# A two-layer diffusion transformer block: TensorE's order in the attention stage written in the source, and both heads' scores in one tile of three PSUM banks

## The chip, the core and the metric

The kernel runs on one core of a Trainium2 chip. The metric is the device time of one execution in microseconds (us). The core's engines run beside each other and meet at semaphores: TensorE (PE, its weight loads apart as PEld), VectorE (DVE), ScalarE (ACT), GpSimd (POOL) and SyncE (SP), which issues the DMAs. TensorE writes its results to PSUM, 8 banks of 512 float32 columns on 128 partitions; VectorE and ScalarE read them there. Each engine works its instructions off in order, so an instruction that waits holds up all behind it on its engine.

## The reference, cut to what matters

Two layers over 512 latent and 256 context tokens, width 1024. One projection of the normed tokens feeds attention (8 query heads, 2 key heads of 64), a pooling branch, a Fourier branch, and a sigmoid gate for each of the three. The attention that the change touches:

```python
h = modulate(rms_norm(x, norm_mix[l]), sh1, sc1)
k, v, q, u, f, gt = jnp.split(h @ w_in[l], IN_SPLITS, axis=-1)
q = apply_rope(q, cos, sin); k = apply_rope(k, cos, sin)
# per query block of 128: own block and its neighbours, |distance| <= 128, and all 256 context keys
s_all = concatenate([where(valid, q @ k_band, NEG_INF), q @ k_ctx, sink]) # scaled by 1/8
p = softmax(s_all)
o = p_lat @ v_band + p_ctx @ v_ctx
y = (g_a * (o @ w_br_attn) + g_p * (pool(u) @ w_br_pool) + g_f * (fourier(f) @ w_br_four))
x = x + g1 * (y @ w_out)
```

In the first layer the context tokens are queries too and read context keys alone. In the second they only give keys and values.

## The kernel before

Activations lie transposed, features on the partitions and the 768 tokens along the columns. A weight tile of 128x1024 comes by one DMA (`wraw`) and is split in two parts of a shorter format, `whi` on ACT (L323) and `wlo` mostly on DVE (L324). A projection runs in steps over the contraction (k steps), each of three matmuls (L346: high x high, high x low, low x high), 512 columns for the latent tokens and 256 for the context, into a PSUM bank from `bank()` (`mp`, or `mm` in stages that have it).

The attention stage of a layer takes the four query tiles t (two heads each) and the query blocks n: 24 units in layer 0 (six blocks, two of them context), 16 in layer 1. A query tile is projected, copied out of PSUM on ACT (L541), rotated (L544 to L547, one of them on GpSimd) and split into high and low parts (L559, L560). A unit then goes like this:

- scores (L602 to L614): for each head, two matmuls against 256 context keys, two against the band of 256 or 384 latent keys, and one or two matmuls that add a mask. A context unit has the first two alone. A unit is 512 or 640 columns wide, or 256 for context;
- softmax: the maximum on DVE (L617), a few small operations (L621, L623), the exponential on ACT (L627) with its sum read off, and the normalisation on DVE (L634);
- turning: each 128 columns of probabilities are transposed on TensorE into the one `tp` bank (L649), four at a time, and copied to SBUF by ACT or DVE (L651, L653);
- values: matmuls of 128 columns for both heads into the `pv` bank (L658), copied out by ACT (L662).

`attn_q` runs two query tiles at a time, and a gate with its Fourier branch (`br_gate`: 8 of them, "filler") is emitted after every third unit in layer 0 and every second in layer 1. The program order is only a start: a scheduler orders the instructions of every engine by its own costs, TensorE's too, so that projections come between the parts of a unit. PSUM in this stage: `sc` has two tiles of two banks, one for each head's scores (L599, `bufs` 2), `tp` and `pv` one bank each, and `mp` two for projections.

Of the kernel before, what the change touches and what calls it, by code (L numbers as in the profile page):

```python
# [17 lines left out]
P = 128  # L18
# [17 lines left out]
SBB = dict(p=2, pt=3)  # L36
# [8 lines left out]
    + tuple((s, (i,), (6, 7)) for i in range(3) for s in "LC"),  # L45
)
# [19 lines left out]
def _plan(l):  # L66
# [12 lines left out]
    fill, gf = [], gates("w_brf", 18, 4)  # L79
    for m in range(8):  # L80
        fill.append([next(gf) for _ in range(1 + (m % 4 == 0))])
    blocks, per = (6, 3) if l == 0 else (4, 2)
    unit = 0
    for half in range(2):
        yield from tiles(6 + 2 * half, 7 + 2 * half)
        for _ in range(2 * blocks):
            unit += 1
            if unit % per == 0 and fill:
                yield from fill.pop(0)
    for f in fill:  # L90
        yield from f
# [17 lines left out]
class Lazy:  # L109
# [6 lines left out]
    def __getitem__(self, i):  # L116
        if self.t[i] is None:
            self.t[i] = self.make()
        return self.t[i]


class Kern:
# [26 lines left out]
    def phase(self, ps, sb):  # L149
        for c in reversed(self.scopes):  # L150
            c.__exit__(None, None, None)
        self.scopes = []
        self.nph += 1
        if ps:
            self.pst, self.sbt = ps, sb
            self.scopes = [
                self.tc.tile_pool(name=f"ps{self.nph}", bufs=1, space=bass.MemoryType.PSUM),
                self.tc.tile_pool(name=f"tp{self.nph}", bufs=1),
            ]
# [358 lines left out]
    def br_gate(self, l, m, mg, br, hs, ls, gh, gl, streams, y, first, steps=0):  # L518
        nc = self.nc
        outs = self.in_tile(l, mg, gh, gl, streams)  # L520
        w, wof = br
        for (b, c0, c1, ps) in outs:
# [4 lines left out]
            self.mm3(pb, w, wof, hs, ls, (c0, c1))  # L527
# [5 lines left out]
        if steps:  # L533
            self.step(last, steps)

# [14 lines left out]
    def attn_q(self, l, t, hs, ls, streams):  # L550
        nc = self.nc
        outs = self.in_tile(l, 6 + t, hs, ls, streams)
        c1 = max(o[2] for o in outs)
        r = self.rope(outs)
        qs = self.slots(2)
        for h in range(2):
            own, oth = (slice(0, 64), slice(64, 128)) if h == 0 else (slice(64, 128), slice(0, 64))
            q = qs[h][:, 0 : c1]
            nc.scalar.copy(q[own], r[own, :c1])  # L559
            nc.vector.tensor_tensor(q[oth], r[own, :c1], q[own].bitcast(F32), ALU.subtract)  # L560
        return qs
# [24 lines left out]
    def scores(self, l, t, n, qs, ka, kb):  # L586
        nc = self.nc
        ps, mx = [], self.small(2)
        if n < 4:
            b0, b1 = max(n - 1, 0), min(n + 1, 3)  # L590
            q0 = n * P
            bl = (b1 - b0 + 1) * P
        else:
            q0 = n * P
            bl = 0
        k0 = b0 * P if n < 4 else 0
        w = bl + CT
        for h in range(2):
            s = self.bk("sc", 1024)[:, 512 - bl : 512 + CT]  # L599
            q = qs[h][:, q0 : q0 + P]  # L600
            cx = s[:, bl:w]
            nc.tensor.matmul(cx, q, ka[h][:, T : N], start=True, stop=False)  # L602
            nc.tensor.matmul(cx, q, kb[h][:, T : N], start=False, stop=True)
            if bl:
                bd = s[:, 0:bl]
# [29 lines left out]
        chunks = ([b0 + j for j in range(bl // P)] if bl else []) + [4, 5]  # L635
        return pr, chunks, q0

    def pv(self, st, vs, o):
        nc = self.nc
        pr, chunks, q0 = st  # L640
        nch = len(chunks)
        pts = []
        for h in range(2):
            pt = self.tmp("pt", 640)
            for j0 in range(0, nch, 4):
                j1 = min(j0 + 4, nch)
                tpb = self.bk("tp", (j1 - j0) * P)
                for j in range(j0, j1):
                    nc.tensor.transpose(tpb[:, (j - j0) * P : (j - j0 + 1) * P], pr[h][:, j * P : (j + 1) * P], self.ident)  # L649
                if (h + j0 // 4) % 2 == 0:  # L650
                    nc.scalar.copy(pt[:, j0 * P : j1 * P], tpb)  # L651
                else:
                    nc.vector.tensor_copy(pt[:, j0 * P : j1 * P], tpb)  # L653
            pts.append(pt)
        po = self.bk("pv", P)
        for j, c in enumerate(chunks):
            for h in range(2):
                nc.tensor.matmul(  # L658
                    po[64 * h : 64 * h + 64, :], vs[:, c * P + 64 * h : c * P + 64 * h + 64],
                    pts[h][:, j * P : (j + 1) * P], start=(j == 0), stop=(j == nch - 1), tile_position=(0, 64 * h),  # L660
                )
        nc.scalar.copy(o[:, q0 : q0 + P], po)  # L662

    def layer(self, l, xs, streams, h=None, after=None):
# [95 lines left out]
        self.phase(dict(sc=2, tp=1, pv=1), SBB)  # L760
        o = self.slots(4, F32)
        gf = iter(range(8))
        wf = [None]

        def filler():
            m = next(gf, None)
            if m is None:
                return
            if m % 4 == 0:
                wf[0] = self.weights("w_brf", l, m // 4)  # L770
            br = (wf[0], lambda k, mm=m: ((mm % 4) * 2 + k) * P)
            self.br_gate(l, m, 18 + m, br, fhi, flo, hs, ls, streams, y[m], False)

        nblk = ncol // P
        units = 0
        per = 3 if nblk > 4 else 2
        for half in range(2):
            ts = (2 * half, 2 * half + 1)
            qs = {t: self.attn_q(l, t, hs, ls, streams) for t in ts}
            prev = None  # L780
            for t in ts:
                for n in range(nblk):
                    st = (self.scores(l, t, n, qs[t], ka, kb), o[t])
                    if prev:
                        self.pv(prev[0], vs, prev[1])
                    prev = st
                    units += 1
                    if units % per == 0:
                        filler()
# [303 lines left out]
```

## Time and profile before

| | |
|---|---|
| median of 3 runs | 1897.43 us (1896.26 to 1898.76) |
| profiled execution, first to last instruction (span) | 1894.8 us |
| median less span | 2.6 us |
| TensorE busy | 1848.8 us, 98% of the span |
| DVE / ACT busy | 65% / 36% |
| attention stage, layer 0, first score to last value product | 205 to 402 us |
| attention stage, layer 1 | 1257 to 1399 us |
| TensorE's granted clock, mean | 0.992 |

The page gives no time of the profiled execution apart from its span; the 2.6 us stand for what lies around it. A start time in a timeline is in us from the span's start. "Idle before, releaser" is time an engine stood before an instruction, and what ended it. TensorE's records are pipelined, so one matmul's pace is read from start to start and not from its length.

### The profile page before, as it was taken

The numbers are of one execution on the slowest core, as the hardware profiler recorded it, in microseconds if no ns is written. First come the engines' busy times: TensorE is split into PE (matmuls) and PEld (weight loads), VectorE is DVE, ScalarE is ACT, GpSimd is POOL, SyncE is SP. The second block draws the span as 40 slices with busy tenths as digits, with TensorE's granted clock in tenths as the row PEclk, the third lists the DMA queues.
The fourth block names the chain that finished last, engine by engine and source line by source line (L and its number), as shares of the span: only waits on it lengthen the run. The fifth ranks groups of instructions, "written<-read, shape, count | busy, mean of one in ns | idle before, by whom it ended". The sixth has DMA issues, their size and how long they took to land. (4 is left out here: it accounts for less than half of the span.)

```text
span 1894.8 us, 26908 instructions
## 1 busy us (share of the span) xinstructions
PE 1848.8 (98%) x10584; PEld 1569.8 (83%) x10584; DVE 1222.7 (65%) x2313; ACT 679.4 (36%) x1132; POOL 143.2 (8%) x102
## 2 busy tenths in 40 slices
PE   6999999999999999999999999999999999999997
PEld 4888877788888888888888888877778988888887
DVE  5687655557758995757566676556753776556556
ACT  4332444432234331313232234344443444233333
POOL 2000101012100000000000031010112200000003
PEclk8999999999999999999999999999999999999998
DMA  9244101024542442323233343321123623222233
GB/s 358 90 143 146 46 23 56 23 74 142 169 150 99 147 132 80 122 89 123 89 123 100 111 146 101 104 78 46 51 70 100 203 91 99 95 99 96 99 99 114
DMA packets 75998, 205.09 MB, mean 108 GB/s; under 512 B 8288, under 2 KB 15712, under 8 KB 75744
## 3 DMA queue, kind: packets, MB, share of 16 engines
q1 hardware_dynamic: 75872, 203.38, 33.1%
q8 instruction: 83, 1.36, 0.3%
q14 instruction: 43, 0.35, 0.1%
HBM read 199.15 MB, written 4.19 MB: 107 GB/s over the span
## 5 line engine op out<-in xcount | busy, mean ns | idle before, releaser
L346 PE MATMUL mm<-slot,whi 128*128 128x512 f32 (+1 forms) x3468 | 895.8, 348 | 7.7 <-DVE slot L886 2.7
L346 PEld LDWEIGHTS mm<-slot,whi 128*128 128x128 f32 x3468 | 609.0, 191 | 89.6 <-DVE slot L886 3.1
L346 PE MATMUL mp<-slot,whi 128*128 128x512 f32 (+1 forms) x2404 | 643.8, 353 | 3.0 <-ACT tg L525 1.5
L346 PE MATMUL mm<-slot,wlo 128*128 128x512 f32 (+1 forms) x1734 | 600.2, 346 | 0.0
L346 PEld LDWEIGHTS mp<-slot,whi 128*128 128x128 f32 x2404 | 418.3, 189 | 64.3 <-issue 6.6
L323 ACT CAST whi<-wraw 128x1024 fp32r<-128x1024 f32 x260 | 272.7, 1049 | 539.2 <-PE mm L346 309.4
L324 DVE TENSOR_TENSOR wlo<-wraw,whi 128x1024 fp32r<-128x1024 f32 x245 | 304.3, 1242 | 246.4 <-ACT whi L323 238.7
L346 PE MATMUL mp<-slot,wlo 128*128 128x512 f32 (+1 forms) x1202 | 421.5, 351 | 1.0 <-POOL wlo L324 1.0
L346 PEld LDWEIGHTS mm<-slot,wlo 128*128 128x128 f32 x1734 | 330.9, 191 | 40.1 <-DVE wlo L324 0.6
L346 PEld LDWEIGHTS mp<-slot,wlo 128*128 128x128 f32 x1202 | 227.4, 189 | 31.8 <-issue 4.3
L294 DVE SCALAR_TENSOR_TENSOR junk<-wmod,cb 128x512 f32<-128x512 f32 x256 | 177.4, 693 | 7.8 <-DMA wmod<-in_w_mt_dram 3.8
L886 DVE SCALAR_TENSOR_TENSOR slot<-mm,mod,slot 128x512 f32<-128x512 f32 (+1 forms) x109 | 66.8, 616 | 62.7 <-PE mm L346 62.7
L324 POOL TENSOR_TENSOR wlo<-wraw,whi 128x1024 fp32r<-128x1024 f32 x15 | 36.8, 2455 | 878.8 <-ACT whi L323 878.8
L532 POOL TENSOR_TENSOR slot<-slot,tg 128x512 f32<-128x512 f32 (+1 forms) x48 | 62.2, 1296 | 408.7 <-DVE tg L531 375.8
L835 DVE SCALAR_TENSOR_TENSOR cp<-mm,p,cp 128x511 f32<-128x511 f32 (+2 forms) x122 | 79.2, 650 | 17.5 <-ACT cp L834 15.6
L627 ACT ACTIVATE p<-sc,sm 128x512 f32<-128x512 f32 (+2 forms) x80 | 54.9, 687 | 32.7 <-PE tp L649 21.0
L658 PE MATMUL pv<-pt,slot 128*64 128x128 f32 x640 | 64.3, 283 | 0.4
L834 ACT ACTIVATE cp<-mm,p 128x512 f32<-128x512 f32 (+1 forms) x60 | 36.8, 613 | 57.6 <-PE mm L346 57.6
L617 DVE TENSOR_REDUCE sm<-sc 128x1 f32<-128x512 f32 (+2 forms) x80 | 53.5, 683 | 6.0 <-PE sc L614 6.0
L658 PEld LDWEIGHTS pv<-pt,slot 128*64 128x64 f32 x640 | 41.2, 136 | 17.8 <-issue 8.2
L653 DVE COPY pt<-tp 128x512 f32<-128x512 f32 (+2 forms) x56 | 30.1, 537 | 39.6 <-PE tp L649 39.5
L649 PE MATMUL tp<-p,p 128*128 128x128 f32 x320 | 54.7, 277 | 0.9 <-ACT pt L651 0.9
(157 smaller groups left out, 1323.8 us busy)
## 6 DMA issues: line engine op xcount, KB each, us to landing
wraw<-in_w_up_dram SPq DMA_DIRECT2D x88, 512.0 KB, 3.5
wmod<-in_w_mt_dram SPq DMA_DIRECT2D x160, 256.0 KB, 3.0
wraw<-in_w_in_dram SPq DMA_DIRECT2D x68, 512.0 KB, 3.5
wraw<-in_w_dn_dram SPq DMA_DIRECT2D x56, 512.0 KB, 3.4
wraw<-in_w_out_dram SPq DMA_DIRECT2D x32, 512.0 KB, 3.5
slot<-in_w_m_dram SPq DMA_DIRECT2D x20, 384.0 KB, 7.5
wraw<-in_w_bra_dram SPq DMA_DIRECT2D x8, 512.0 KB, 3.6
slot<-in_xc_dram SPq DMA_DIRECT2D x8, 256.0 KB, 4.5
```

Of the source, the lines that this page charges most:

```text
L294: nc.vector.scalar_tensor_tensor(junk[:, 0:512], w, 1.0, self.cb[:, b, hs], ALU.mult, ALU.mult, accum_out=acc[:, b * 2 + h : b * 2 + h + 1])
L323: self.cpy = nc.scalar.copy(hi, raw)
L324: (eng or nc.vector).tensor_tensor(lo, raw, hi.bitcast(F32), ALU.subtract)
L346: self.mm = self.nc.tensor.matmul(out, ww, xx, start=(k == 0 and i == 0), stop=(k == n - 1 and i == 2))
L532: nc.gpsimd.tensor_tensor(y[:, c0 : c1], y[:, c0 : c1], tg[:, c0:c1], ALU.add)
L617: nc.vector.tensor_reduce(mx[:, h : h + 1], s, AX.X, ALU.max)
L627: nc.scalar.activation(p[:, :w], ps[h], AF.Exp, bias=ngm[:, h : h + 1], scale=0.125, accum_out=den[:, h : h + 1])
L649: nc.tensor.transpose(tpb[:, (j - j0) * P : (j - j0 + 1) * P], pr[h][:, j * P : (j + 1) * P], self.ident)
L658: nc.tensor.matmul(po[64 * h : 64 * h + 64, :], vs[:, c * P + 64 * h : c * P + 64 * h + 64], pts[h][:, j * P : (j + 1) * P], start=(j == 0 ...
L834: nc.scalar.activation(c[:, c0:c1], ps, AF.Copy, scale=cw(1))
L835: tap = lambda d, src, i: nc.vector.scalar_tensor_tensor(c[:, d], src, cw(i), c[:, d], ALU.mult, ALU.add)
L886: nc.vector.scalar_tensor_tensor(xv, ps, g2(m, b), xv, ALU.mult, ALU.add)
```

## The change

All of it is in the attention stage.

- TensorE's order is taken from the scheduler and written in the source (`manual_schedule` for PE in `attention`); the other engines are ordered as before. For each unit: its scores, then the previous unit's transposes in groups of up to four, then that unit's value products in one piece.
- Query and gate projections become generators that yield after each k step. `Beside` deals them out: `go(left/5)` after each transpose group, after them, and after the value products. A unit with 10 transposes has three groups, so five calls; one with 8 has two, so four; one with 4 has three calls. `need(t)` takes all steps up to query tile t when its first unit comes.
- The scores of both heads go to one tile of three banks: head 0 has its band in the first and its context in the middle bank, head 1 its context in the middle and its band in the third. `sc` has one such tile, and the bank that is freed becomes `mm`, a third one for projections.
- The probabilities' buffers go from 2 to 4, the turned ones from three of 640 columns to one of 1280. Transposes of the two heads share a group. Pools release at tile level (`reuse_waits="tile"`).
- The order in which weights are loaded (`_plan`) follows the same list, `BESIDE`.

```diff
+BESIDE = (
+    ("q", 0), ("g", 0), ("q", 1), ("g", 1), ("g", 2), ("q", 2), ("g", 3), ("g", 4), ("q", 3), ("g", 5), ("g", 6), ("g", 7),
+)
+class Beside:
+    def go(self, n):
+        self.left += n
+        while self.left > 0:
+            s = next(self.steps, None)
+            if s is None:
+                return
+            self.take(s)
+            self.left -= 1
+    def need(self, key):
+        while key not in self.done:
+            self.take(next(self.steps))
+            self.left -= 1
...
-        full = 1024 if tag == "sc" else 512
+        full = 1536 if tag == "sc" else 512
...
+        sc = self.bk("sc", 1536)
+        band = list(range(b0, b1 + 1))
+        chunks = (band + [4, 5], [4, 5] + band)
         for h in range(2):
-            s = self.bk("sc", 1024)[:, 512 - bl : 512 + CT]
             q = qs[h][:, q0 : q0 + P]
-            cx = s[:, bl:w]
+            s = sc[:, 512 - bl : 512 + CT] if h == 0 else sc[:, 512 + CT : 1024 + bl]
+            cx, bd = (s[:, bl:w], s[:, 0:bl]) if h == 0 else (s[:, 0:CT], s[:, CT:w])
...
+    def turn_p(self, st):
+        items = [(h, j) for h in range(2) for j in range(len(chunks[h]))]
+        pt = self.tmp("pt", 10 * P)
+        for i0 in range(0, len(items), 4):
+            part = items[i0 : i0 + 4]
+            tpb = self.bk("tp", len(part) * P)
...
+            (nc.vector.tensor_copy if i0 == 4 else nc.scalar.copy)(pt[:, i0 * P : (i0 + len(part)) * P], tpb)
+            yield pt
...
+    def attention(self, l, ka, kb, vs, o, hs, ls, fhi, flo, y, streams, nblk):
...
+        bs.go(18 * ns)
+        total = (3 * 8 + 7 * 10) * ns
+        size = lambda n: 0.6 if n >= 4 else 1.0
+        per = total / (sum(size(n) for _, n in units) + 0.5)
+        for t, n in units + [(None, None)]:
+            left = per * (0.5 if t is None else size(n))
...
+                bs.need(t)
+                st = self.scores(l, t, n, qs[t], ka, kb)
+            if prev:
+                pst, po = prev
+                g = self.turn_p(pst)
+                for pt in g:
+                    bs.go(left / 5)
+                bs.go(left / 5)
+                self.pv(pst, pt, vs, po)
+                bs.go(left / 5)
...
-        self.phase(dict(sc=2, tp=1, pv=1), SBB)
+        self.phase(dict(sc=1, tp=1, pv=1, mm=1), SBB)
...
+        with self.tc.manual_schedule(engines={mybir.EngineType.PE}):
+            self.attention(l, ka, kb, vs, o, hs, ls, fhi, flo, y, streams, ncol // P)
```

Three places on TensorE show how the order moves. In the rows, `sc` is a scores tile, `tp` and `pv` the banks of the transposes and value products, `mp` and `mm` those of the projections; "waits" names the engine or queue whose semaphore an instruction waits for. The first is a unit of layer 0 with 640 columns, its scores. Before:

```order
L602 MATMUL sc<-slot 128x256 [waits Activation_49]
L603 MATMUL sc<-slot 128x256
L606 MATMUL sc<-slot 128x384
L607 MATMUL sc<-slot 128x384
L614 LDWEIGHTS identb
L614 MATMUL sc<-maskb,identb 128x128
L614 LDWEIGHTS identb
L614 MATMUL sc<-maskb,identb 128x128
L602 MATMUL sc<-slot 128x256 [waits Activation_49]
L603 MATMUL sc<-slot 128x256
L606 MATMUL sc<-slot 128x384
```

And of the change:

```order
L638 MATMUL sc<-slot 128x256 [waits PE_49,Activation_49]
L639 MATMUL sc<-slot 128x256
L641 MATMUL sc<-slot 128x384
L642 MATMUL sc<-slot 128x384
L649 LDWEIGHTS identb
L649 MATMUL sc<-maskb,identb 128x128
L649 LDWEIGHTS identb
L649 MATMUL sc<-maskb,identb 128x128
L638 MATMUL sc<-slot 128x256 [waits DVE_49]
L639 MATMUL sc<-slot 128x256
L641 MATMUL sc<-slot 128x384
```

Head 1's first matmul (the second row that has a wait) waited for ACT before, which had read an older unit out of the same tile; now it waits for DVE, and that is the maximum of head 0 of the same unit (L652, L617 before), the DVE instruction that reads the middle bank. The second place is the end of a unit's turning in the same layer, and its value products. Before:

```order
L649 MATMUL tp<-p_87,p 128x128 [waits DVE_49,Activation_49]
L649 MATMUL tp<-p_87,p 128x128 x3
L658 MATMUL pv<-pt,slot 64x128
L346 MATMUL mp<-slot,whi 128x256
L346 MATMUL mp<-slot,wlo 128x256
L346 MATMUL mp<-slot,whi 128x256
L602 MATMUL sc<-slot 128x256 [waits Activation_49]
L603 MATMUL sc<-slot 128x256
L606 MATMUL sc<-slot 128x384
L658 MATMUL pv<-pt,slot 64x128 [waits DVE_49]
L658 MATMUL pv<-pt,slot 64x128 x6
L607 MATMUL sc<-slot 128x384
```

And of the change:

```order
L365 MATMUL mp<-slot,whi 128x256 x2
L365 MATMUL mp<-slot,wlo 128x256
L365 MATMUL mp<-slot,whi 128x256 x2
L365 MATMUL mp<-slot,wlo 128x256
L693 MATMUL pv<-pt,slot 64x128
L693 MATMUL pv<-pt,slot 64x128 [waits DVE_49]
L693 MATMUL pv<-pt,slot 64x128 x6
L365 MATMUL mp<-slot,whi 128x256 x2
L365 MATMUL mp<-slot,wlo 128x256
L638 MATMUL sc<-slot 128x256 [waits Activation_49]
```

The value products stood in two pieces, the second between two score matmuls of the next unit; now they stand in one, behind projection steps that are complete. The third is the second unit of the last query tile (t = 3) of layer 0, at the transposes of the unit before it and what follows. Before:

```order
L614 LDWEIGHTS identb
L614 MATMUL sc<-maskb,identb 128x128
L649 MATMUL tp<-p_87,p 128x128 [waits DVE_49,PE_49]
L649 MATMUL tp<-p_87,p 128x128
L346 MATMUL mp<-slot,whi 128x256 [waits DVE_49]
L346 MATMUL mp<-slot,whi 128x256
L346 MATMUL mp<-slot,wlo 128x256
L346 MATMUL mp<-slot,whi 128x256 x2
L346 MATMUL mp<-slot,wlo 128x256
L649 MATMUL tp<-p_87,p 128x128 [waits Activation_49]
L649 MATMUL tp<-p_87,p 128x128
L658 MATMUL pv<-pt,slot 64x128
```

And of the change:

```order
L649 MATMUL sc<-maskb,identb 128x128
L638 MATMUL sc<-slot 128x256 [waits DVE_49,Activation_49]
L639 MATMUL sc<-slot 128x256
L641 MATMUL sc<-slot 128x256
L642 MATMUL sc<-slot 128x256
L649 LDWEIGHTS identb
L649 MATMUL sc<-maskb,identb 128x128
L681 MATMUL tp<-p_87,p 128x128 [waits PE_49]
L681 MATMUL tp<-p_87,p 128x128 x3
L693 MATMUL pv<-pt,slot 64x128 [waits Activation_49]
L693 MATMUL pv<-pt,slot 64x128 x3
L638 MATMUL sc<-slot 128x256 [waits PE_49,Activation_49]
```

Before, projection matmuls stood between the transposes and the value products; now none does, and the next unit's scores come straight behind. All 48 matmuls of query tile 3 stand right ahead of the scores of its first unit.

## Rows read from the trace of the kernel before

**Rows 1.** the page: the span, and busy time of each engine.
```profile
span 1894.8 us, 26908 instructions
...
PE 1848.8 (98%) x10584; PEld 1569.8 (83%) x10584; DVE 1222.7 (65%) x2313; ACT 679.4 (36%) x1132; POOL 143.2 (8%) x102
```

**Rows 2.** windows: stretch, length, busy PE, PEld, DVE, ACT, POOL, then PE's clock.
```profile
205.00:402.00 197.00, 193.08 (x1315) 152.04 (x1313) 113.88 (x270) 86.19 (x219) 19.54 (x18) 1.00 0.11 35
1257.30:1399.00 141.70, 139.96 (x906) 106.06 (x907) 97.85 (x195) 66.96 (x154) 16.62 (x11) 1.00 0.15 48
1130.00:1137.00 7.00, 4.33 (x26) 3.87 (x25) 7.00 (x12) 4.15 (x6) 2.37 (x1) 0.83 0.37 145
```

**Rows 3.** weight loads' waits, layer 0's attention: us, times, longest.
```profile
PEld tp L649 <- ACT pt L651: 5.4, 20, 0.7
...
PEld pv L658 <- ACT pt L651: 0.4, 1, 0.4
```

**Rows 4.** the same view, attention of layer 1.
```profile
PEld tp L649 <- ACT pt L651: 3.1, 15, 0.2
...
PEld sc L602 <- ACT sm L629: 0.3, 2, 0.2
```

**Rows 5.** groups by form, 200 to 402 us: count, busy, mean ns, idle.
```profile
L617 DVE TENSOR_REDUCE sm<-sc 128x1 f32<-128x640 f32 x16 | 13.0, 823 | 3.4 <-PE sc L614 3.4
L627 ACT ACTIVATE p<-sc,sm 128x640 f32<-128x640 f32 x16 | 12.7, 794 | 3.5 <-PE tp L649 2.7 <-DVE sm L621 0.9
L653 DVE COPY pt<-tp 128x512 f32<-128x512 f32 x16 | 11.1, 691 | 16.6 <-PE tp L649 16.6
L617 DVE TENSOR_REDUCE sm<-sc 128x1 f32<-128x512 f32 x16 | 10.3, 682 | 0.0
L651 ACT COPY pt<-tp 128x512 f32<-128x512 f32 x16 | 9.4, 587 | 26.9 <-PE tp L649 26.9
L617 DVE TENSOR_REDUCE sm<-sc 128x1 f32<-128x256 f32 x16 | 6.6, 411 | 0.0
```

**Rows 6.** timeline (start, length), layer 1: rope, then a unit's first scores.
```profile
1252.46 0.74 DVE L544 STREAM_SHUFFLE cp<-cp 128x512 f32<-128x512 f32 x1
...
1255.46 0.39 PE L346 MATMUL mp<-slot,wlo 128*128 128x512 f32 x1
...
1255.69 0.39 PE L346 MATMUL mp<-slot,whi 128*128 128x512 f32 x1
...
1257.31 0.36 PE L602 MATMUL sc<-slot 128*128 128x256 f32 x1 [1.24 <-DVE slot L560]
...
1257.86 0.23 PE L614 MATMUL sc<-maskb,identb 128*128 128x128 bf16 x1
...
1258.13 0.69 DVE L617 TENSOR_REDUCE sm<-sc 128x1 f32<-128x512 f32 x1 [0.24 <-PE sc L614]
```

**Rows 7.** timeline, layer 0: one copy out of a transpose group.
```profile
382.37 0.48 PE L346 MATMUL mp<-slot,wlo 128*128 128x512 f32 x1
...
382.65 0.69 DVE L653 COPY pt<-tp 128x512 f32<-128x512 f32 x1 [0.66 <-PE tp L649]
...
383.40 0.33 PE L649 MATMUL tp<-p,p 128*128 128x128 f32 x1
```

**Rows 8.** timeline, layer 0: first and a late step of a rope.
```profile
300.80 0.59 ACT L541 COPY cp<-mp 128x512 f32<-128x512 f32 x1 [4.73 <-PE mp L346]
...
305.93 1.94 DVE L560 TENSOR_TENSOR slot<-cp,slot 64x768 fp32r<-64x768 f32 x2
```

**Rows 9.** timeline, layer 0: a product of probabilities and values in two pieces.
```profile
225.27 1.09 PE L658 MATMUL pv<-pt,slot 128*64 128x128 f32 x16
...
226.30 0.51 PE L346 MATMUL mp<-slot,whi 128*128 128x256 f32 x2
...
226.73 0.43 PE L658 MATMUL pv<-pt,slot 128*64 128x128 f32 x2
...
227.09 0.39 PE L346 MATMUL mp<-slot,wlo 128*128 128x256 f32 x1
```

More of the change, by code (lines that the diff above doesn't have):

```diff
@@ L35 @@
 SBA = dict(cv=1, st=4)
-SBB = dict(p=2, pt=3)
+SBB = dict(p=4, pt=1)
 LS = (0, T)
@@ L78, in _plan @@
         yield from tiles(4, 5)
[L79 to L91, printed above, removed]
+    gf = gates("w_brf", 18, 4)
+    for kind, j in BESIDE:
+        if kind == "q":
+            yield ("w_in", l, 6 + j)
+        else:
+            yield from (next(gf) for _ in range(1 + (j % 4 == 0)))
     for m in range(8):
@@ L119, in __getitem__, with __init__, take @@
         return self.t[i]
+class Beside:
+    def __init__(self, steps):
+        self.steps, self.left, self.done = steps, 0.0, set()
+    def go(self, n):
[6 more added lines that the diff above has]
+            self.left -= 1
+    def take(self, s):
+        if s is not True:
+            self.done.add(s)
+    def need(self, key):
+        while key not in self.done:
+            self.take(next(self.steps))
+            self.left -= 1
 class Kern:
@@ L516, in fourier, with mm3_steps, tile_steps, gate_steps @@
             self.split(o[:, 0:n], hi[:, c0:c1], lo[:, c0:c1])
-    def br_gate(self, l, m, mg, br, hs, ls, gh, gl, streams, y, first, steps=0):
+    def mm3_steps(self, out, w, wof, hs, ls, cols):
+        n = len(hs)
+        for k in range(n):
+            self.mmk(out, w, k, wof(k), hs, ls, cols, n)
+            yield True
+    def tile_steps(self, outs, l, m, hs, ls, streams):
+        w = self.weights("w_in", l, m)
+        for (b, (c0, c1)) in streams:
+            ps = self.bank(c1 - c0)
+            yield from self.mm3_steps(ps, w, lambda k: k * P, hs, ls, (c0, c1))
+            outs.append((b, c0, c1, ps))
+    def gate_steps(self, l, m, mg, br, hs, ls, gh, gl, streams, y, first, steps=0):
         nc = self.nc
-        outs = self.in_tile(l, mg, gh, gl, streams)
+        outs = []
+        yield from self.tile_steps(outs, l, mg, gh, gl, streams)
         w, wof = br
@@ L526, in br_gate @@
             pb = self.bank(n)
-            self.mm3(pb, w, wof, hs, ls, (c0, c1))
+            yield from self.mm3_steps(pb, w, wof, hs, ls, (c0, c1))
             if first:
@@ L759, in layer @@
         ka, kb, vs = kv if l else self.attn_kv(l, hs, ls, both)
-        self.phase(dict(sc=2, tp=1, pv=1), SBB)
+        self.phase(dict(sc=1, tp=1, pv=1, mm=1), SBB)
         o = self.slots(4, F32)
[L762 to L789, printed above, removed]
-            self.pv(prev[0], vs, prev[1])
-        for _ in range(8):
-            filler()
+        with self.tc.manual_schedule(engines={mybir.EngineType.PE}):
+            self.attention(l, ka, kb, vs, o, hs, ls, fhi, flo, y, streams, ncol // P)
         self.phase(dict(mm=6 - NP, aux=2), SBA)
```

76 lines of the change are left out of this document (42 added, 34 removed).

## The prediction

> **What bounds the kernel now.** The page first: TensorE is busy 1848.8 of 1894.8 us [rows 1], so whatever lengthens its queue lengthens the kernel. Then the windows of the two attention stages, the only place the change touches: TensorE is busy 193.08 of 197.00 us and 139.96 of 141.70, at a clock of 1.00, while DVE is busy 114 and 98 and ACT 86 and 67 [rows 2]. The reader is to see that TensorE stands idle for only 3.92 + 1.74 = 5.7 us in both stages together; idle time can't give back more. A finer view is what its weight loads wait for: eight groups apart from "issue" add up to 15.6 us in layer 0 (5.4 to 0.4), seven to 9.8 in layer 1 (3.1 to 0.3) [rows 3, 4], 25.4 together. Such a wait partly lies beside a matmul that still runs, so what they cost is between 5.7 and 25.4.
>
> Everything off TensorE is covered now because the scheduler lays projections into every gap. So the question is which waits the written order leaves uncovered.
>
> **The sum.** No matmul is added or taken away, and the DVE and ACT work is the same to within copy shapes; weights load in a like order, and I cost that at nothing, since DMAs and splits run two tiles ahead of TensorE. The terms:
>
> *1. Head 1 waits for head 0's maximum.* The order shows head 1's first score matmul waiting for DVE in each of the 40 units, right behind head 0's last matmul, with nothing between. TensorE is in order, so nothing fills the time. Per unit: from the start of the last mask matmul to the start of the maximum 0.27 us (1257.86 to 1258.13) [rows 6]; the maximum itself 0.82, 0.68 or 0.41 for 640, 512 or 256 columns [rows 5]; from the end of a DVE instruction to TensorE's next start 0.06 (382.65 + 0.69 to 383.40) [rows 7]; less the pace that the mask matmul had anyway, 0.05, or 0.12 for a context matmul (half of the 0.23 between two 512-column matmuls, 1255.46 to 1255.69 [rows 6]). That is 1.10, 0.96 and 0.62. Layer 0 has eight units of each kind, 21.4 us; layer 1 eight of 640 and eight of 512, 16.5. **+38**. It presumes that DVE is free. It is busy 58% and 69% of the stages [rows 2], and if the maximum found it in the midst of an instruction (0.3 us on average, six units in ten) it would be 40 x 0.6 x 0.3 = 7 more; since in the trace the maxima start as soon as a score ends or behind one another, I take 3 of these. **+3**.
>
> The Trainium skill has a rule on just this ("PSUM — Partial Sum Buffer", section "PSUM bank collisions raise a hardware error"): two engines must not be on one bank at the same time, whatever columns they touch, and software has to keep them apart by semaphores. By that rule the wait can't be left out as long as the middle bank holds both heads, and the sum holds +41 here; without it this term would be nothing. No row of before has two heads in one bank, so no trace bears on it yet.
>
> *2. Copies between the transpose groups.* With one `tp` bank, a group waits for the copy of the group before: 0.28 from the transposes' end to the copy's start (382.37 to 382.65), the copy, 0.69 on DVE or 0.59 on ACT for 512 columns [rows 5], and 0.06, so 0.93 to 1.03. Between the groups now stand whole k steps: 0.35 each at 256 columns and 0.69 at 512. In layer 0 there are 48 copies (three, two or one in a unit), 40 in layer 1. Most in layer 0 have two steps of 256 (0.7) or two of 512 (1.4) beside them: 36 copies lose about 0.09 on average, 3.3; behind five copies around the first units of t = 3 there is no step left, 0.84 each, 4.2. In layer 1, with one or two steps of 512, I take 0.16 for each of the 40, 6.4. **+14**, between 4 (only the bare ones) and 28 (each some 0.3 short).
>
> *3. The rope is exposed.* The deal-out falls short: a unit with 8 transposes calls `go(left/5)` four times and one with 4 three times, so the steps lag behind and query tile 3 is taken whole by `need` right ahead of its scores. Before, its chain lay beside projections. Layer 0: from ACT's copy at 300.80 to the split's end at 305.93 + 1.94 is 7.1 us [rows 8], the first head's half done 1.0 earlier, plus 0.3 to get started, and 24 context matmuls (24 x 0.12 = 2.9) beside it: 3.5 exposed. Layer 1 has no context part: 0.3 + 0.59 for the copy + 4.85 (1252.46 to 1257.31) [rows 6] = 5.7. **+9**, between 5 (half of the chain covered by something that I don't see) and 13 (with a split of weights in DVE's way, once in each layer).
>
> *4. Units without filler.* After that forced projection the debt makes `go` yield nothing for two to three units of layer 0 and one of layer 1. Their softmax is then covered only by 10 transposes and 10 value products, about 2.4 us against 3.5 (0.27 + 0.82 for the maximum, two exponentials of 0.79 [rows 5], and some 0.8 of small operations between them, my estimate): about 1.1 short, four times. **+4** (2 to 8: two such units or seven).
>
> *5. Value products in one piece.* There were 96 runs of them in the order, now there are 40. The price of a run stands in one place: eight matmuls from 225.27 to 226.30, then two projection matmuls, a lone value product, and the next at 227.09 [rows 9]. In 0.79 us two projection matmuls (0.23) and one value product (1.03 / 8 = 0.13) were done, so the run cost 0.43. The lower end is its exit alone, 227.09 − 226.73 − 0.13 = 0.23. I take 0.31, between them, since many of the runs were broken at a wait, which the next term has. 56 fewer: **−17** (−13 to −24).
>
> *6. Waits that go.* The waits of before belong to an order that goes; between 5.7 and 25.4, I take the middle: **−15**.
>
> Sum: 38 + 3 + 14 + 9 + 4 − 17 − 15 = +36. The span would be 1894.8 + 36 = 1930.8 us, and with the 2.6 us that lie around it 1933.4; that is the median's 1897.4 plus 36. The terms' lower ends (38 + 0 + 4 + 5 + 2 − 24 − 25.4) make 0, the upper ones (38 + 7 + 28 + 13 + 8 − 13 − 5.7) +75; they won't all fall to one side, and I put the likeliest case at 1912 to 1955.
>
> **The rivals.**
>
> *The clock falls* (0.10). In this trace TensorE's clock stayed at 1.00 through both stages, but where it stood idle it did not: in 1130 to 1137 it was busy 4.33 of 7.00 us at a mean clock of 0.83 [rows 2], so in part at 1.2 instead of 2.4 GHz. The waits of terms 1 to 4 make 68 us of idle pieces in what would be 375 us. Against it: each piece is about 1 us, and matmuls stand on both sides. Were the clock low in the two sparse stretches at t = 3, some 12 us of TensorE work each, that would be +10 to +25: 1943 to 1958. The Trainium skill names such a mechanism ("TensorE: Matmul & The Clock Gate", section "A second HAM failure mode: psum-queue depth-cycling"): small idle gaps between matmul groups that cycle through PSUM make the clock swing. By that rule the stages would show a mean clock below 1.00.
>
> *Softmax becomes the chain* (0.05). With one `sc` tile the next unit's scores wait for this unit's last exponential. If ACT and DVE, with copies and splits in their queues, run some 1 us later than TensorE's work in every unit and not in four, that is 36 more: about 1970. Against it: a unit of layer 0 has 4 us of filler beside its 2.4.
>
> *The written order wins* (0.07). Not slower: head 1's wait costs little, as TensorE's queue has loads to do meanwhile and the maximum is done early, and fragments and waits go at their full price. Then 14 + 9 + 4 − 24 − 25 = −22: about 1875. It decides when the wait costs less than 0.5 us a unit. For it: 25.4 us of waits are on record. Against it: an in-order engine and a dependency with nothing behind it.
>
> *It evens out* (0.04): every gain at its upper and every cost at its lower end, 1897.
>
> **Chances.** Forecast 0.74, clock 0.10, softmax 0.05, written order 0.07, even 0.04. A measurement of this kernel tells 0.2% from no change, 3.8 us. So slower 0.89, same 0.04, faster 0.07. The range 1909 to 1955 leaves out the written order, the even case and softmax, and the edges of the others.
>
> **What would show it.** In the changed profile: waits of the score matmul of head 1 (L638) for DVE's L652, 40 of them at 0.6 to 1.1 us, about 40 us in all; TensorE's busy share in both stages down from 98 to about 85 in a hundred; fewer and longer runs of value products; a gap of 3 to 6 us ahead of the first unit of t = 3 in both layers; transposes (L681) that wait for copies (L682). I would be wrong if those 40 waits add up to less than 20 us, if the stages come out shorter than 197 and 142 us, or if the clock there is below 0.95.

## The result, and the profile after

The changed kernel takes 1962.84 us (median of 4 runs, 1961.15 to 1964.3) against 1898.09 before (median of 4): a ratio of 1.0343, 95% interval 1.0328 to 1.0357. It is slower, by 65 us where 36 were forecast, and outside the range of 1909 to 1955. The page of the changed kernel, its span, TensorE's line, the granted clock in 40 slices, and the chain's engines:

```profile
span 1962.5 us, 26842 instructions
...
PE 1854.3 (94%) x10584; PEld 1576.7 (80%) x10584; DVE 1223.2 (62%) x2289; ACT 680.1 (35%) x1132; POOL 144.0 (7%) x102
...
PEclk8999999799999999999999999999899999999998
...
PE 35%; DVE 3%; issue 1%; ACT 1%; POOL 1%; POOLq 0%; DVEq 0%; ACTq 0%
```

TensorE is busy for 94% where it was 98% [rows 1], and its clock falls to 7 and 8 tenths in slices that lie in the attention stages; its mean is 0.979 where it was 0.992. By stretch, TensorE's busy time first after the length, the clock third from the end (1.00 is 2.4 GHz, 0.50 is 1.2 GHz): both attention stages with their tails, and the scores at the start of t = 3 in layer 0.

```profile
200.00:460.00 260.00, 223.74 (x1473) 182.45 (x1473) 128.92 (x274) 94.89 (x231) 24.08 (x21) 0.94 0.11 35
1290.00:1460.00 170.00, 139.34 (x894) 104.60 (x893) 98.59 (x191) 67.27 (x156) 14.89 (x11) 0.94 0.12 37
361.00:379.00 18.00, 13.74 (x64) 9.78 (x64) 8.14 (x19) 5.52 (x15) 0.00 (x0) 0.53 0.15 43
```

TensorE stands idle for 260 − 223.74 = 36.3 and 170 − 139.34 = 30.7, 66.9 us, where it was 5.7 [rows 2, stages without their tails]; over the whole span, idle time went from 1894.8 − 1848.8 = 46.0 to 1962.5 − 1854.3 = 108.2. The clock's mean there is 0.94 where it was 1.00. While it was busy, that costs 0.06 x (223.74 + 139.34) = 21.8 us; added up over windows of 1 us it is 20.2. What TensorE's matmuls waited for (us, times, longest) in these two stretches, layer 0:

```profile
PE sc L638 <- DVE sm L652: 21.6, 24, 2.1
PE sc L638 <- DVE slot L598: 3.3, 1, 3.3
PE tp L681 <- ACT pt L682: 2.6, 5, 0.8
PE mm L365 <- ACT tg L558: 2.5, 1, 2.5
PE tp L681 <- DVE pt L682: 1.7, 3, 0.8
```

and layer 1:

```profile
PE sc L638 <- DVE sm L652: 15.4, 16, 2.1
PE sc L638 <- DVE slot L598: 9.7, 3, 6.7
PE tp L681 <- ACT pt L682: 3.5, 3, 2.0
PE tp L681 <- DVE pt L682: 1.5, 4, 0.9
```

All 40 waits of head 1 for head 0's maximum are there, 21.6 + 15.4 = 37.0 us of idle TensorE. The rope's are 3.3 and 9.7. This is how the waits look at t = 3 in layer 0, in the timeline (start, length):

```profile
357.30 0.28 PE L365 MATMUL mm<-slot,wlo 128*128 128x256 f32 x1
...
359.87 1.94 DVE L598 TENSOR_TENSOR slot<-cp,slot 64x768 fp32r<-64x768 f32 x2
...
360.87 0.39 PE L638 MATMUL sc<-slot 128*128 128x256 f32 x1 [3.30 <-DVE slot L598]
...
361.26 0.42 PE L641 MATMUL sc<-slot 128*128 128x256 f32 x1
...
361.48 0.42 PE L642 MATMUL sc<-slot 128*128 128x256 f32 x1
...
361.70 0.33 PE L649 MATMUL sc<-maskb,identb 128*128 128x128 bf16 x1
362.07 0.69 DVE L652 TENSOR_REDUCE sm<-sc 128x1 f32<-128x512 f32 x1 [0.26 <-PE sc L649]
...
362.91 0.55 PE L638 MATMUL sc<-slot 128*128 128x256 f32 x1 [0.88 <-DVE sm L652]
...
371.30 1.06 PE L681 MATMUL tp<-p,p 128*128 128x128 f32 x4
...
372.45 0.59 ACT L682 COPY pt<-tp 128x512 f32<-128x512 f32 x1 [5.02 <-PE tp L681]
...
373.09 1.12 PE L681 MATMUL tp<-p,p 128*128 128x128 f32 x4 [0.73 <-ACT pt L682]
```

The last projection matmul stands at 357.30, the rope's last step on DVE runs from 359.87, and the first score starts at 360.87, after 3.30 us of idle time. Right behind it the score matmuls go 0.22 apart (0.12 at a clock of 1.00, as e4 below shows): the window from 361 to 379 has a clock of 0.53, so it is 1.2 GHz most of the time. Head 1's first score waits from the mask at 361.70 to 362.91 for a maximum of 0.69. Further down two transpose groups stand with a copy of 0.59 between them and nothing else.

About 13.5 of the 20.2 us that the clock costs lie at t = 3, behind the two long gaps. The other 6.7 lie behind four waits of 2.0 to 2.5 us, two of them head 1's longest waits for the maximum (the 2.1 of the lists); a wait of 2.3 us for a rope was followed by no lower clock. Two of those places, TensorE busy throughout at 0.50, behind the 2.5 us for tanh (L558) and behind layer 1's longest wait for the maximum:

```profile
426.00:429.00 3.00, 3.00 (x9) 2.33 (x8) 0.02 (x1) 0.00 (x0) 0.73 (x1) 0.50 0.05 16
1300.00:1303.00 3.00, 3.00 (x9) 2.33 (x8) 2.42 (x4) 1.20 (x1) 1.27 (x1) 0.50 0.38 150
```

### The profile page after: what moved, and what is told of

Its sections match the earlier page's. It is cut to its first block, busy times and chain, and to the rows that moved or that the text cites. A ratio compares the mean times of both kernels' runs of the same rounds, so it can differ in the third digit from the quotient of the medians.

```text
span 1962.5 us, 26842 instructions
## 1 busy us (share of the span) xinstructions
PE 1854.3 (94%) x10584; PEld 1576.7 (80%) x10584; DVE 1223.2 (62%) x2289; ACT 680.1 (35%) x1132; POOL 144.0 (7%) x102
## 5 line engine op out<-in xcount | busy, mean ns | idle before, releaser
L365 PE MATMUL mm<-slot,whi 128*128 128x512 f32 (+1 forms) x3764 | 982.0, 350 | 10.5 <-ACT slot L419 3.5
L365 PEld LDWEIGHTS mm<-slot,whi 128*128 128x128 f32 x3764 | 658.6, 191 | 102.9 <-ACT slot L419 4.1
L365 PE MATMUL mm<-slot,wlo 128*128 128x512 f32 (+1 forms) x1882 | 654.0, 348 | 0.0
L365 PE MATMUL mp<-slot,whi 128*128 128x512 f32 (+1 forms) x2108 | 557.9, 353 | 2.5 <-ACT slot L369 1.4
L365 PEld LDWEIGHTS mp<-slot,whi 128*128 128x128 f32 x2108 | 367.6, 191 | 55.2 <-issue 5.1
L365 PE MATMUL mp<-slot,wlo 128*128 128x512 f32 (+1 forms) x1054 | 366.7, 348 | 1.0 <-POOL wlo L343 1.0
L652 DVE TENSOR_REDUCE sm<-sc 128x1 f32<-128x512 f32 (+2 forms) x80 | 55.1, 689 | 83.5 <-PE sc L649 71.0
L932 DVE SCALAR_TENSOR_TENSOR slot<-mm,mod,slot 128x256 f32<-128x256 f32 (+1 forms) x103 | 62.8, 613 | 61.7 <-PE mm L365 61.5
L638 PE MATMUL sc<-slot 128*128 128x256 f32 x80 | 28.9, 361 | 50.4 <-DVE sm L652 37.0
L682 ACT COPY pt<-tp 128x512 f32<-128x512 f32 (+1 forms) x56 | 29.4, 526 | 109.3 <-PE tp L681 99.3
L681 PEld LDWEIGHTS tp<-p,p 128*128 128x128 f32 x320 | 37.2, 149 | 25.3 <-ACT pt L682 15.1
```

Source lines behind the costliest of these rows:

```text
L365: self.mm = self.nc.tensor.matmul(out, ww, xx, start=(k == 0 and i == 0), stop=(k == n - 1 and i == 2))
L652: nc.vector.tensor_reduce(mx[:, h : h + 1], s, AX.X, ALU.max)
L681: nc.tensor.transpose(tpb[:, i * P : (i + 1) * P], pr[h][:, j * P : (j + 1) * P], self.ident)
L682: (nc.vector.tensor_copy if i0 == 4 else nc.scalar.copy)(pt[:, i0 * P : (i0 + len(part)) * P], tpb)
L932: nc.vector.scalar_tensor_tensor(xv, ps, g2(m, b), xv, ALU.mult, ALU.add)
```

## The experiments

Times are medians beside the kernel before, which took 1896.6 to 1898.1 in all comparisons. The runs e1 to e5 and e7 change one thing in the changed kernel. The edits are shown cut, and that of e1 in words.

**e1, context scores of both heads first.**

```diff
-        for h in range(2): context scores, band scores, masks, maximum
+        for h in range(2): context scores
+        for h in range(2): band scores, masks, maximum
```

> One edit to the changed kernel (1962.8 us): both heads' context scores come first, then head 0's band, then head 1's band. Head 1's band lies in the third bank, which head 0's maximum does not read. Theory A (the wait comes from the shared bank): after both context parts nothing of head 1 touches a bank that head 0's maximum reads, the 40 waits of head 1 for DVE (in the changed kernel 38 us on the weight loads) go, and with them some 40 us: 1915 to 1930 us. Rival B (the wait comes from the one tile, in which the maximum is written between the two heads' matmuls): the 32 latent units wait as before, now ahead of head 1's band; only the 8 context units lose their wait of 0.6 each: 1953 to 1962 us.

Measured: 1962.0 us, ratio 1.0344 (1.0329 to 1.036), no change. The waits in layer 0, and one of them with the maximum ahead of it:

```profile
PE sc L643 <- DVE sm L654: 16.3, 16, 2.1
```

```profile
225.42 0.82 DVE L654 TENSOR_REDUCE sm<-sc 128x1 f32<-128x640 f32 x1 [0.68 <-PE sc L651]
226.29 0.44 PE L643 MATMUL sc<-slot 128*128 128x384 f32 x1 [0.92 <-DVE sm L654]
```

Head 1's band waits for a maximum that reads other banks: 16 waits in each layer, one for each latent unit, as long as before. The context units' waits did go (21.6 − 16.3 = 5.3 us); the clock took them back, with 28 us lost to it in both stages where it was 20, added up in the same way. So the bank is not what makes head 1 wait. What is left is the one tile, in which the program writes a read between two writes; e7, with a tile for each head, bears that out.

**e2, both maxima behind both heads' scores.**

```diff
-            nc.vector.tensor_reduce(mx[:, h : h + 1], s, AX.X, ALU.max)   # in the heads' loop
+        for h in range(2):                                               # behind it
+            nc.vector.tensor_reduce(mx[:, h : h + 1], ps[h], AX.X, ALU.max)
```

> One edit to the changed kernel: both maxima are written behind the score matmuls of both heads, so that head 1's matmuls no longer come behind a read of the tile; head 0's maximum starts later by head 1's matmuls, 0.4 to 0.7 us. Theory A (the 40 waits cost what they last): they go, about 40 us and a few more where the clock had fallen behind them: 1908 to 1925 us, waits of scores for DVE's maximum under 2 us. Rival B (the softmax chain becomes the bound): the chain is 0.6 us longer in each unit, and the time comes back as waits of the transposes for DVE's normalisation and of the next scores for ACT's exponential: 1935 to 1955 us.

Measured: 1918.9 us, ratio 1.012 (1.0105 to 1.0135): 44 us gone by moving one line, though the middle bank still holds both heads. No wait for the maximum is left. The waits of layer 1, and the clock behind the rope's gap of 3.3 us in layer 0:

```profile
PE sc L638 <- DVE slot L598: 9.7, 3, 6.8
PE tp L682 <- DVE pt L683: 6.0, 4, 4.5
```

```profile
340.00:351.00 11.00, 8.37 (x39) 6.36 (x39) 6.09 (x12) 3.34 (x9) 0.00 (x0) 0.53 0.28 89
```

The rope costs its 9.7 as before. Transposes wait 6.0 us for copies on DVE, 1.5 in the changed kernel; 4.5 of them are one copy that stood on DVE behind steps of a rope, a split of weights and the two maxima. The clock costs 11.8 us in both stages where it was 20.2, added up in the same way: behind the same gap in layer 0 the clock is down for about 10 us where it was 17 and, soon after, another 7, while in layer 1 it is down for 14 in both. So a part of the 44 is clock. Theory A holds.

**e3, steps dealt out over the calls there are.**

```diff
-                for pt in g:
-                    bs.go(left / 5)
+                share = left / (-(-2 * len(pst[1][0]) // 4) + 2)
+                for pt in self.turn_p(pst):
+                    bs.go(share)
```

(and the two other calls with `share`).

> One edit to the changed kernel: a unit's projection steps are dealt out over the calls that it really has (five, four or three) and not always by fifths, so that query tile 3 is done before it is needed and no unit stands without steps. Theory A (the clock falls because of the long gap for the rope and the bare units behind it): the gaps of 3.3 and 6.7 us shrink below 1 us each, the mean clock at t = 3 goes back to 0.95 or more (20 us are lost in the stages to the clock, 13 to 14 of them at t = 3), and 20 to 28 us go: 1935 to 1943 us. Rival B (the many short waits for the maximum lower the clock): the gaps shrink, some 9 us, but the clock still falls in both layers: 1950 to 1956 us.

Measured: 1943.6 us, ratio 1.025 (1.0235 to 1.0265), 19 less. Waits of layer 1, and the windows at t = 3 in both layers:

```profile
PE sc L638 <- DVE sm L652: 15.7, 16, 2.1
PE sc L638 <- DVE slot L598: 5.3, 2, 4.6
```

```profile
350.00:400.00 50.00, 42.06 (x288) 34.18 (x289) 26.60 (x60) 21.68 (x54) 1.99 (x2) 0.97 0.10 32
1380.00:1430.00 50.00, 40.66 (x267) 30.59 (x265) 26.78 (x57) 20.14 (x49) 4.76 (x3) 0.93 0.11 37
```

In layer 0 the rope's wait is gone and the clock is back at 0.97 with all 24 waits for the maximum in place (what is missing lies behind a wait of 3.0 us for tanh); in layer 1, 4.6 us of one rope wait are left (6.7 before), and there the clock still falls, to 0.93. Theory A for layer 0, half of it for layer 1.

**e4, idle time filled with matmuls that nobody needs.**

```diff
+                if (t, n) == (3, 0):
+                    fill = self.bank(512)
+                    for _ in range(14 if l == 0 else 28):
+                        self.nc.tensor.matmul(fill, kb[0][:, 0:P], ka[0][:, 0:T], start=True, stop=True)
+                    self.nc.vector.tensor_copy(self.small(2)[:, 0:1], fill[:, 0:1])
```

> The changed kernel with matmuls of 512 columns whose results nobody uses, right ahead of the scores of the first unit of t = 3: 14 in layer 0 (3.2 us) and 28 in layer 1 (6.4 us), as long as the gaps in which TensorE waits for the rope there (3.3 and 6.75 us). They add no time of their own as long as they stay within the gaps. Theory A (the gap itself lowers the clock for the units behind it): the clock stays at 1.00 in those units, and the 13 us that the clock costs there go, less a few for the bare units: 1948 to 1957 us. Rival B (the sparse units behind the gap lower it): the clock falls all the same, somewhat later, and the time stays within 3 us of 1962.8.

Measured: 1951.1 us (1946.2 to 1959.9), ratio 1.0303 (1.0278 to 1.0327): 12 us faster with more work. TensorE in layer 0 at the place shown above, both windows at t = 3, and a window at the start of layer 1's stage:

```profile
353.87 3.36 PE L728 MATMUL mp<-slot 128*128 128x512 f32 x14
357.35 0.39 PE L638 MATMUL sc<-slot 128*128 128x256 f32 x1
357.57 0.28 PE L639 MATMUL sc<-slot 128*128 128x256 f32 x1
357.69 0.28 PE L641 MATMUL sc<-slot 128*128 128x256 f32 x1
...
357.93 0.23 PE L649 MATMUL sc<-maskb,identb 128*128 128x128 bf16 x1
359.09 0.36 PE L638 MATMUL sc<-slot 128*128 128x256 f32 x1 [0.93 <-DVE sm L652]
...
364.60 0.39 PE L638 MATMUL sc<-slot 128*128 128x256 f32 x1 [1.16 <-DVE sm L652]
```

```profile
350.00:400.00 50.00, 40.34 (x294) 31.70 (x292) 28.73 (x62) 21.35 (x53) 3.36 (x3) 1.00 0.10 32
1380.00:1430.00 50.00, 43.45 (x281) 33.08 (x277) 29.17 (x59) 20.97 (x49) 4.27 (x3) 1.00 0.11 37
1284.00:1287.00 3.00, 3.00 (x10) 2.52 (x11) 1.08 (x2) 0.00 (x0) 0.00 (x0) 0.50 0.59 180
```

The 14 matmuls fill the gap, and the scores behind it go 0.12 apart from the second on (0.22 in the changed kernel), with the same bare units and the same waits of 0.7 to 1.2 us between them. The clock at t = 3 is 1.00 in both layers. So in this run the waits of about 1 us did not lower the clock by themselves; with the gap filled, the 13 us that it had cost at t = 3 were gone. Two of head 1's waits were of 2.1 us: behind the one in layer 0 the clock stayed up, behind the one at 1283.8 in layer 1 it fell (the last row). The trace is that of the run of 1946.2 us, with a mean clock of 0.993; the other three, 1950.7 to 1959.9 us, had 0.985 to 0.988 and left no trace. So the clean clock is shown for one execution, and where the others lost theirs stays open.

**e5, the scheduler's order on the changed kernel.**

```diff
-        with self.tc.manual_schedule(engines={mybir.EngineType.PE}):
-            self.attention(l, ka, kb, vs, o, hs, ls, fhi, flo, y, streams, ncol // P)
+        self.attention(l, ka, kb, vs, o, hs, ls, fhi, flo, y, streams, ncol // P)
```

> The changed kernel with one part undone: TensorE's order in the attention stage comes from the scheduler again; the single tile, the place of the maxima, the order in which steps are emitted and the buffers stay. Head 1 still waits for head 0's maximum in each unit, but the order now has one to eight rows of projections and often transposes between the two heads. Theory A (the waits cost only because the written order leaves nothing between): they are covered, the clock stays at 1.00, 1895 to 1908 us. Rival B (one tile and the late query tile 3 cost by themselves): more than 1925 us.

Measured: 1889.2 us, ratio 0.9957 (0.9942 to 0.9971), faster than the kernel before. Windows of both stages, and the weight loads' wait for the maximum in layer 0:

```profile
200.00:450.00 250.00, 244.91 (x1650) 202.34 (x1649) 151.90 (x341) 102.51 (x242) 34.46 (x28) 1.00 0.17 56
1250.00:1460.00 210.00, 207.52 (x1222) 163.13 (x1221) 119.62 (x219) 90.62 (x187) 31.91 (x19) 1.00 0.20 66
```

```profile
PEld sc L638 <- DVE sm L652: 1.3, 5, 0.5
```

And the same line of the changed kernel:

```profile
PEld sc L638 <- DVE sm L652: 24.8, 23, 2.3
```

The tile is still one and the dependency still there; with other work between the heads it costs 1.3 us of weight-load waits there in place of 24.8. All of the loss, and more, is this written order; e12, with the maxima moved and a second transpose bank, has a written order that does not lose.

**e6, e2 and e3 together; e7, a tile for each head as before; e8, e6 with query tiles 2 and 3 one gate earlier.**

```diff
+        chunks = (band + [4, 5], band + [4, 5])                          # e7
+            s = self.bk("sc", 1024)[:, 512 - bl : 512 + CT]              # e7, in the heads' loop
+        self.phase(dict(sc=2, tp=1, pv=1), SBB)                          # e7
+    ("q", 0), ("g", 0), ("q", 1), ("g", 1), ("q", 2), ("g", 2), ("g", 3), ("q", 3), ("g", 4), ...   # e8
```

> The two edits that helped, together: both maxima behind both heads' scores (alone 44 us less than the changed kernel's 1962.8) and steps dealt out over the calls there are (19 less). Theory A (they take away different waits): 1962.8 - 44 - 19 = 1900, 1897 to 1904 us, with the mean clock in the stages above 0.98. Rival B (the longer softmax chain needs the steps that were bunched): 1908 to 1918 us, with the transposes waiting for DVE.

> One edit to the changed kernel: each head's scores go to a tile of two banks of their own, as before the change, and the third projection bank goes; TensorE's order stays written in the source, maxima stay between the heads. Theory A (the single tile is what made head 1 wait): the 40 waits go as with the late maxima, and the next unit's head 0 can start as soon as its own exponential is done: 1905 to 1920 us. Rival B (the projections miss their third bank more): waits of projections for the gates' tanh and products take back 10 us or more: 1925 to 1940 us.

> e6 with query tiles 2 and 3 projected one gate earlier each, so that 10 to 15 k steps lie between a query tile's last matmul and the scores that need its rope. In the run with even shares alone 6.1 us in layer 1 were still waits for the rope. Theory A (these are left because the rope's 5.7 us are longer than the steps behind it): 5 to 7 us less than e6 and the clock of layer 1 at 1.00 throughout: 1890 to 1897 us. Rival B (they only move the step debt to the last units): within 3 us of e6.

Measured: e6 1902.4 us, ratio 1.0026 (1.0016 to 1.0036), within theory A's 1897 to 1904, so the two edits take different waits. e7 1913.1, ratio 1.0085 (1.0069 to 1.01): the waits go with the tiles too, 50 us, in A's range; projections wait 5.4 us for the gates' products in layer 0 (1.1 in the changed kernel), which goes with the third bank that they lost:

```profile
PE mp L365 <- DVE tg L564: 5.4, 6, 1.5
```

e8 1894.9, ratio 0.9984 (0.9975 to 0.9994), 7.5 below e6: waits for the rope in layer 1 fell from 5.3 to 0.7 us, and the clock's cost in both stages from 6.6 to 3.4.

**e9, the scheduler with late maxima; e10, with even shares and earlier query tiles; e11, with a tile for each head.** The edits are those above.

> The scheduler's order (1889.2 us) with both maxima behind both heads' scores. Theory A (under the scheduler head 1's wait is covered: 1.3 us of weight-load waits for the maximum in layer 0): nothing to gain, 1886 to 1892 us. Rival B (the waits that the scheduler has to cover cost it other pieces of its order): 3 to 6 us less, 1883 to 1886.

> The scheduler's order with even shares and the earlier query tiles, which gave 19 and 7 us in the written order. Theory A (in the written order they gave what the scheduler does by itself): 1886 to 1892 us, as without them. Rival B (the order in which steps are emitted still matters to the scheduler): 4 us or more to either side.

> The scheduler's order with a tile of two banks for each head as before the change and without the third projection bank: what is left of the change is the steps dealt out by k, the transposes' groups over both heads, the buffers and the release of pools. Theory A (the 8 us below the kernel before come from these): 1887 to 1892 us. Rival B (they come from the third projection bank): 1895 to 1899 us, as before the change.

Measured: e9 1880.4, ratio 0.9906 (0.989 to 0.9923); e10 1877.8, ratio 0.9894 (0.9879 to 0.9909). Expectation A missed for both, 9 and 11 us too high; e10 fits its rival B, and e9 lies below its rival's 1883 to 1886 too. TensorE's idle time in 200:450 and 1250:1460 was 7.6 us in e5 and is 6.1 and 5.5, so idle time is not where the gain lies; but the scheduler breaks fewer runs. Its order has 86 runs of scores and 78 of value products in e5, 44 and 65 in e9, 83 and 56 in e10 (73 and 96 before). That the runs are the cause is argued from these counts. e11 1887.6, ratio 0.9946 (0.9931 to 0.9961): the three banks and the third projection bank are not what makes e5 faster than before. Which of the parts that are left does it, no run shows.

**e12, e8 with two banks for transposes; e13, e12 with the value products cut in two; e14, e12 by the scheduler; e15, e8 by the scheduler.**

```diff
+        self.phase(dict(sc=1, tp=2, pv=1), SBB)                          # e12, e13, e14
+                bs.go(share / 2)                                         # e13
+                self.pv(pst, pt, vs, po, lambda: bs.go(share / 2))       # called behind the first block
```

> The written order with late maxima, even shares and earlier query tiles (1894.9 us), with two banks for the transposes and two in place of three for projections. In 1894.9 the transposes' weight loads still wait 10 us in layer 0 and 13 in layer 1 for copies out of the one bank. Theory A (that is what is left of the copy term): 8 to 16 us less, 1879 to 1887 us. Rival B (projections wait for their bank instead): 1893 to 1900 us.

> e12 (1882.2 us) with the value products cut behind the first block and half of the steps ahead of them moved in between: 72 runs of value products in the order in place of 40, all else alike. It prices a run, which the prediction took at 0.31 us (0.23 to 0.43) from one place in the trace of before. Theory A (that price holds on average): 32 x 0.31 = 10 us more, 7 to 14: 1889 to 1896 us. Rival B (a run costs about a third of it, the place read was a dear one, so that the prediction's gain of 17 us for 56 runs was some 6): 2 to 5 us more, 1884 to 1887 us.

> e12 (late maxima, even shares, earlier query tiles, two banks for transposes; 1882.2 us in the written order) with the scheduler's order instead: the price of the written order itself once its waits are taken care of. Theory A (what is left of it is waits that a scheduler covers: 16.7 us of TensorE's idle time in the two stretches 200:450 and 1250:1460 of e12 against 5.5 in e10): 8 to 12 us less, 1870 to 1874 us. Rival B (with two banks for projections the scheduler has to break its runs, as before the change): 1876 to 1884 us.

> The scheduler's order with all three edits and the third projection bank, the sum of e9 (9 us below the scheduler alone at 1889.2) and e10 (11 below). Theory A (one gain is from fewer breaks at the scores, 44 runs in place of 86, the other from fewer breaks at the value products, 56 in place of 78; they add up): 1868 to 1872 us. Rival B (both take the same waits): 1875 to 1879 us.

Measured: e12 1882.2, ratio 0.9913 (0.9898 to 0.9928), 13 below e8: the price of the one transpose bank, less what projections lose with their third. e13 1891.4, ratio 0.9966 (0.9954 to 0.9979): 9.2 us for 32 runs, 0.29 each. e14 1870.0, ratio 0.9856 (0.9843 to 0.987); e15 1873.1, ratio 0.987 (0.9856 to 0.9883). The stages of e12, then of e14:

```profile
200.00:450.00 250.00, 239.16 (x1666) 203.00 (x1665) 155.46 (x345) 102.28 (x241) 31.32 (x27) 0.99 0.17 58
1250.00:1460.00 210.00, 204.14 (x1287) 166.90 (x1286) 126.31 (x224) 93.15 (x190) 33.14 (x20) 1.00 0.22 75
```

```profile
200.00:450.00 250.00, 246.22 (x1713) 209.75 (x1712) 161.08 (x361) 103.14 (x242) 32.53 (x28) 1.00 0.19 64
1250.00:1460.00 210.00, 207.78 (x1331) 170.93 (x1330) 129.00 (x222) 94.06 (x189) 34.18 (x21) 1.00 0.24 82
```

With the same edits the scheduler leaves 6.0 us of idle time where the written order leaves 16.7, and is 12 us faster by the medians (8 between the two executions traced, 1877.9 and 1869.6). e14 beats both kernels, by 27 us the one before. e15's gains do not add up in full (1 us above A's 1868 to 1872, below B's 1875).

## Why the prediction missed

The direction, the places and most prices were right; the sum lacked a term, the clock, and held one that wasn't there, most of term 6.

1. *Head 1's wait*: forecast 38 + 3, measured 37.0 us of idle time, 44 with its removal [e2]. The size was right, the cause wrong. The prediction put it down to the middle bank, and drew on the Trainium skill for it ("PSUM — Partial Sum Buffer", section "PSUM bank collisions raise a hardware error"), by which two engines on one bank have to be kept apart. No run here tests that rule. But e1 took the bank away and the wait stayed, and e2 left the bank as it was and the wait went, so it could be left out after all. It comes from one tile and the order in which its reads and writes are written.
2. *Copies*: forecast 14; idle time for them is 2.6 + 1.7 + 3.5 + 1.5 and three smaller ones of value products, 10.6 in all, and e12 takes 13 out of a better kernel.
3. *Rope*: forecast 3.5 + 5.7 at t = 3, measured 3.3 + 6.75 there; with two shorter waits of layer 1 ahead of other query tiles it is 13.0, the upper end.
4. *Bare units*: forecast 4, measured 1.7 as waits for a normalisation and an exponential. What I did not see are projections that wait for tanh or a gate's product, 3.6. Together the waits were forecast at 38 + 3 + 14 + 9 + 4 = 68, and the idle time is 66.9; that the two meet is in part luck, since head 1, the copies and the bare units came out 10 below and the rope and these projections 8 above.
5. *Value products in one piece*: forecast −17 at 0.31 a run; e13 gives 0.29, so −16. (In rows 9 a value product stands as two records, 640 for 320 in the kernel; so x16 are the prediction's eight matmuls.)
6. *Waits that go*: forecast −15, the middle of 5.7 and 25.4. This was wrong. TensorE's idle time was 5.7 us; the rest of the 25.4 of weight-load waits lay beside matmuls that still ran, and the fragments were already paid for in term 5. The pages bear it out: TensorE's busy time grew by 1854.3 − 1848.8 = 5.5 us, and without the clock's 20.2 it fell by 14.7; that is all that terms 5 and 6 gave beyond idle time, where 17 + 9 were forecast. Nine us of the miss.
7. *The clock*. The step that failed most: "the clock falls" stood as a rival, with a chance of 0.10, beside the sum, though its price (10 to 25) was about the 20 us measured. It was no alternative to the forecast. The forecast itself put a gap of 3.5 and of 5.7 us ahead of t = 3, and the row of 1130 to 1137 [rows 2] has a clock of 0.83 with a gap of only 2.00 us in it, which the timeline of the kernel before shows:

```profile
1134.89 0.80 PE L346 MATMUL mm<-slot,whi 128*128 128x256 f32 x2 [2.00 <-DVE slot L886]
```

So the clock was mostly a consequence of term 3, with a part from head 1's two longest waits, and belonged into the sum. The reason given against it, that each piece of idle time is about 1 us, held for most pieces and not for term 3's own.

Put together: idle time 66.9 − 5.7, clock 20.2, runs −16 make +65; the span grew by 67.7. The forecast of +36 lacks the 20 of the clock and has 9 too much in term 6. The Trainium skill's rule ("TensorE: Matmul & The Clock Gate", section "A second HAM failure mode: psum-queue depth-cycling") names many small idle gaps as what makes the clock swing. The trace agrees that it swings, with a mean of 0.94. But e4's trace has all 40 waits and a clock of 1.00 at t = 3, so there it was the long gaps and not the many pieces of about 1 us; the measurement decides.

Of the signs named, the 40 waits came with 37.0 us, the busy share in both stages with 84%, the gaps ahead of t = 3 with 3.3 and 6.75 us, and so did one sign of being wrong, a clock below 0.95. The rivals: the clock fell, but beside the forecast's terms and not in their place, and the time lies above that rival's 1943 to 1958; the written order did not win; softmax as the chain did not come (one wait for an exponential, 0.35 us, in both stages of the changed kernel).

## What to carry to other kernels

Where an order is written by hand for an in-order engine, read it once for each wait and ask what stands between the wait and its releaser; a read that is written between two writes of one tile was such a wait here, and moving it by a line gave 44 us of the 65 that the reordering had cost. A long gap (here 3 to 7 us) is priced twice: by its length, and by the clock of what follows. What an engine's weight loads wait for is not what it loses: of 25.4 us of such waits, 5.7 stood as idle time. Nor does idle time bound what another order can win: e9 and e10 won 9 to 11 us where 7.6 stood idle.

## What the runs showed that I had not expected

Useless matmuls made the kernel 12 us faster by the median [e4]: they ran in time that TensorE would have stood idle, and the clock did not fall behind it. One run of value products costs 0.29 us [e13], so the number of breaks in TensorE's order has a price of its own, beside idle time. And under the scheduler it paid to emit the program in a better order, by 9 to 11 us [e9, e10], although at most 2 us of that came as idle time.
